# A squared-ReLU channel mixer with seven half-size products per block in place of eight

## The chip, the core and the metric

The kernel runs on one NeuronCore of a Trainium2 chip. Its engines work side by side, each through its own queue in order: TensorE (PE; its weight loads are shown as PEld), VectorE (DVE), ScalarE (ACT), GpSimd (POOL), and SyncE (SP), whose queue issues the transfers. The metric is device time in microseconds, the median of several runs.

## The reference

One step of a one-layer encoder over 576 tokens whose output is returned (512 of a prompt and 64 of a sample stream; 16 meta tokens more take part in attention). Two token mixers (differential attention, gated DeltaNet) are merged, projected and added to x. The part that the change touches is the last:

```python
h2 = _rmsnorm(x, p["norm2"])
x = x + jnp.square(jax.nn.relu(h2 @ p["w_up"])) @ p["w_down"]
```

with 1024 features, a hidden width of 4096, all in float32.

## The kernel before

All large products are one stream of tasks on PE. A task takes a block of 256 columns of a weight matrix over 1024 rows. The weights (`wr`, two transfers of 512 KB a task) are split into a high part `wh` (an ACT cast) and the remainder `wl` (a subtraction on DVE or POOL); activations likewise. A product of float32 quality is then three passes: high times high, high times low, low times high (`feat`).

In the channel mixer a task makes 256 features for 576 tokens: two halves of the features by two halves of the tokens, each 8 blocks of rows by 3 passes, that is 4 x 24 = 96 matmuls of a 128x128 weight tile against 288 tokens. There are 16 tasks of `w_up` (`up_task`, PSUM tiles `pg_u`) and 16 of `w_down` (`down_tasks`, `pg_dn`, four quarters of the hidden width by four blocks of features). They are ordered with the first `up` task of the next quarter ahead of a quarter's `down` tasks.

The eviction of an `up` piece is four instructions on 288 tokens: ReLU times the token's norm (DVE, from PSUM to `ur`), a square (ACT), a cast to `uh` (ACT), and the remainder `ul` (DVE). The hidden values have ten buffers of each kind, so a task has many matmuls to go before its predecessor's values are wanted. The eviction of a `down` piece is one DVE addition to the residual `x1`.

Which engine gets what, and when, is decided as the program is written, by `Pace`, an estimate of each engine's time. `stream` puts a step of the next task's weights (`split_hi`, `split_lo`, `load`) between every eight matmuls; `drive` lets the chains (norms, evictions, output) go on beside it; `VG` gives an elementwise operation to DVE or POOL, whichever the estimate has done sooner. The queues are then fixed: an instruction waits in its queue for everything ahead of it. The lines are

```python
QUANTUM = 8     # products between two turns of the chains
wp = Tags(pace, ctx.enter_context(pool("weights")), wh=2, wl=2, wr0=1, wr4=1)
```

`token_norm` finds 1/sqrt of each token's mean square (`n2` tiles, PSUM tiles `pss` and `prs`); `write_y` turns the result back to tokens on PE (`pyo`) and stores it.

## Time and profile before

| | |
|---|---|
| median of 3 runs | 1376.14 us (1373.91 to 1378.1) |
| profiled execution, first to last instruction | 1370.9 us, so 5.2 us less than that median |
| PE busy / PEld busy | 1315.5 us (96%) / 1273.0 us (93%) |
| DVE / ACT / POOL busy | 700.1 us (51%) / 565.8 us (41%) / 260.6 us (19%) |
| channel mixer, first `pg_u` to last `pg_dn` | 951.01 to 1364.89 us: 413.9 us |

Only the mixer's 413.9 us are changed in what they compute; busy shares over the whole span say little about them. The profiled execution has no time of its own beside its span, so sums are made against the span and carried over to the median by the 5.2 us.

### The profile page before, as it was taken

Reading aid. Unit: us, or ns where it says so; the run is one execution under the profiler, and the core shown is the slowest. Engines: PE = TensorE matmul, PEld = TensorE weight load, DVE = VectorE, ACT = ScalarE, POOL = GpSimd, SP = SyncE. Lnnn points to the kernel's source line nnn. Section 1 sums busy time; section 2 is a strip of 40 time slices with the busy share of each in tenths; the row PEclk is TensorE's granted clock in tenths of the full one; section 3 lists DMA queues with packets and bytes.
Section 4 is the critical chain, followed back from the end, with each engine's and each line's share of the span. In section 5 each row is a group of like instructions: output and inputs, shape, how many; then the busy total and the mean of one; then the engine's idle time right before and its main releaser. Section 6 shows DMA issues by size and latency. Waiting matters only on the chain.

```text
span 1370.9 us, 25684 instructions
## 1 busy us (share of the span) xinstructions
PE 1315.5 (96%) x10365; PEld 1273.0 (93%) x10365; DVE 700.1 (51%) x1556; ACT 565.8 (41%) x1368; POOL 260.6 (19%) x244
## 2 busy tenths in 40 slices
PE   3999999999999999998799899999999999999998
PEld 3999999999999999997688799999999999999998
DVE  5766999434377424278867743535332233233232
ACT  3556554433752333355566532323431331331321
POOL 5101422200230000243232101200220220320300
PEclk9999999999999999999999999999999999999999
DMA  6314243522644413774453157532222222222231
GB/s 171 93 47 133 88 126 122 154 91 73 210 120 132 138 59 93 236 225 149 122 172 101 67 171 257 191 98 78 77 87 70 91 93 72 83 93 78 78 110 52
DMA packets 163946, 161.06 MB, mean 117 GB/s; under 512 B 23546, under 2 KB 143628, under 8 KB 163828
## 3 DMA queue, kind: packets, MB, share of 16 engines
...
## 4 chain that ended last, share of the span: by engine, by line
PE 84%; DVE 8%; ACT 4%; DMA 3%; issue 1%; SPq 1%; ACTq 0%; DVEq 0%
PE pg_dn L164 15%; PE pg_u L164 15%; PE pg_a L164 10%; PE pg_d L164 9%; PE pg_g L164 6%; PE pg_z L164 4%; PE pg_o L164 4%; PE pg_ba L164 4%; PE pg_bb L164 3%; PE ppo L164 2%; DVE sc L164 2%; PE po L164 1%; ACT djk L164 1%; PE psc L164 1%; PE pwT L164 1%
## 5 line engine op out<-in xcount | busy, mean ns | idle before, releaser
L164 PE MATMUL pg_dn<-ul,wh_dn 128*128 128x288 f32 x512 | 151.6, 296 | 0.0
L164 PE MATMUL pg_dn<-uh,wh_dn 128*128 128x288 f32 x512 | 151.6, 296 | 0.0
L164 PE MATMUL pg_u<-h2h,wh_u 128*128 128x288 f32 x512 | 151.4, 296 | 0.0
L164 PE MATMUL pg_u<-h2h,wl_u 128*128 128x288 f32 x512 | 151.2, 295 | 0.0
L164 PE MATMUL pg_u<-h2l,wh_u 128*128 128x288 f32 x512 | 151.2, 295 | 0.0
L164 PE MATMUL pg_dn<-uh,wl_dn 128*128 128x288 f32 x512 | 151.1, 295 | 0.0
L164 PE MATMUL pg_a<-wh_a,hh 128*128 128x256 f32 (+1 forms) x480 | 136.3, 284 | 0.9 <-ACT sq L164 0.9
L164 PE MATMUL pg_a<-wh_a,hl 128*128 128x256 f32 (+1 forms) x480 | 136.2, 284 | 0.0
L164 PE MATMUL pg_a<-wl_a,hh 128*128 128x256 f32 (+1 forms) x480 | 135.6, 282 | 0.0
L164 PE MATMUL pg_d<-hl,wh_d 128*128 128x336 f32 (+1 forms) x384 | 116.5, 303 | 0.4 <-DVE hl L164 0.3
L164 PE MATMUL pg_d<-hh,wh_d 128*128 128x336 f32 (+1 forms) x384 | 116.2, 303 | 0.6 <-ACT hh L164 0.5
L164 PE MATMUL pg_d<-hh,wl_d 128*128 128x336 f32 (+1 forms) x384 | 115.9, 302 | 0.0
L164 POOL TENSOR_TENSOR wl_u<-wr_u,wh_u 128x1024 fp32r<-128x1024 f32 x22 | 52.8, 2401 | 260.5 <-ACT wh_u L164 260.5
L164 DVE TENSOR_TENSOR x<-x,pg_dn 128x288 f32<-128x288 f32 x64 | 29.1, 454 | 132.5 <-PE pg_dn L164 132.5
L164 PEld LDWEIGHTS pg_u<-h2h,wh_u 128*128 128x128 f32 x512 | 96.5, 189 | 0.1
L164 PEld LDWEIGHTS pg_u<-h2l,wh_u 128*128 128x128 f32 x512 | 96.5, 189 | 0.0
L164 PEld LDWEIGHTS pg_u<-h2h,wl_u 128*128 128x128 f32 x512 | 96.5, 188 | 0.0
L164 PEld LDWEIGHTS pg_dn<-uh,wl_dn 128*128 128x128 f32 x512 | 96.3, 188 | 0.0
L164 PEld LDWEIGHTS pg_dn<-uh,wh_dn 128*128 128x128 f32 x512 | 96.1, 188 | 0.0
L164 PEld LDWEIGHTS pg_dn<-ul,wh_dn 128*128 128x128 f32 x512 | 96.1, 188 | 0.0
L164 PEld LDWEIGHTS pg_a<-wh_a,hh 128*128 128x128 f32 (+1 forms) x480 | 86.6, 180 | 2.1 <-ACT sq L164 1.5
L164 PEld LDWEIGHTS pg_a<-wh_a,hl 128*128 128x128 f32 (+1 forms) x480 | 86.7, 181 | 0.7 <-issue 0.6
...
## 6 DMA issues: line engine op xcount, KB each, us to landing
wr_u<-in_w_up_dram SPq DMA_DIRECT2D x32, 512.0 KB, 3.7
wr_dn<-in_w_down_dram SPq DMA_DIRECT2D x32, 512.0 KB, 3.5
wr_d<-in_w_in_dram SPq DMA_DIRECT2D x24, 512.0 KB, 4.1
wr_a<-in_w_in_dram SPq DMA_DIRECT2D x24, 512.0 KB, 4.1
wr_g<-in_w_in_dram SPq DMA_DIRECT2D x16, 512.0 KB, 4.7
...
wr_z<-in_w_in_dram SPq DMA_DIRECT2D x8, 512.0 KB, 3.8
```

The costliest lines, as they stand in the source:

```text
L164: r = f(*a, **kw)
```

## The change

Each task is read as a product of 2x2 blocks: two halves of the block's columns by two interleaved halves of its rows (weights a11, a12, a21, a22), and two halves of the rows by two halves of the tokens. Seven products of sums of these (Strassen's algorithm in Winograd's form) take the place of eight. Each of the seven is 4 blocks of rows by 3 passes, 12 matmuls of 128x128 against 288 tokens: 84 a task.

- The seven products are called by number and run in the order 1, 6, 7, 5, 2, 4, 3. They use four PSUM tiles: `pa` (1, then 2 added to it), `pb` (6), `pc` (7, then 4), `pd` (5, then 3). A tile is evicted before its second product is added.
- Weights (`seven_steps`): four sums of 512 elements (`s1` to `s4`, into the tile `s` and in place in `wr`), then 3 1/2 casts and 3 1/2 subtractions of 1024 where there were 2 of each. They come as two blocks: the first (products 1, 6, 7, 5) is made during the task before, the second (2, 4, 3) during the task itself.
- Activations (`combine`): each pair of feature tiles is kept as seven pieces. Four results in `r` give three pieces at once (a cast and a subtraction of 864); four subtractions of 288 in place give the other four (a cast and a subtraction of 1152).
- An `up` task now evicts seven products into `uw` and `r`, one set of buffers for all tasks. When product 3 is out, the chain `squares` does ReLU and squares on 576 elements twice and then `combine`. Product 5 of the next task is evicted only after that chain has been written (`after`).
- The order is four `up` tasks, then four `down` tasks, four times. The first `up` task, and the first `down` task of each group, take the last of the four pairs late (`LATE`).
- Some constants and scratch tiles move to a pool that ends before the merge; there are no other changes of substance before the mixer.

```diff
+        def seven_steps(i):
...
+            def s1():
+                (_, a21), (_, a22) = quarters(0), quarters(1)
+                st["s"] = late["wx"].tile([P, 4, 256], F32, name=f"s_{tasks[i].nm}", tag="ws")
+                VG(2.1, 512).tensor_tensor(st["s"][:, :, 0:128], a21, a22, ALU.add)
+            def s2():
+                VG(2.1, 512).tensor_tensor(st["s"][:, :, 128:256], st["s"][:, :, 0:128], quarters(0)[0], ALU.subtract)
+            def s3():
+                a11, a21 = quarters(0)
+                VG(2.1, 512).tensor_tensor(a21, a11, a21, ALU.subtract)
+            def s4():
+                a12 = quarters(1)[0]
+                VG(2.1, 512).tensor_tensor(a12, a12, st["s"][:, :, 128:256], ALU.subtract)
+            def hi(b, a, x, n=256):
+                if a == 0:
+                    block(i)
+                S.copy(wts[i][b]["wh"][:, 4 * a:4 * a + 4, 0:n], x()[:, :, 0:n])
+            def lo(b, a, x, n=256, tag=None):
+                w = wts[i][b]
+                lower(w["wl"][:, 4 * a:4 * a + 4, 0:n], x()[:, :, 0:n], w["wh"][:, 4 * a:4 * a + 4, 0:n])
+                if tag:
+                    load(tag)
+            r0, r1, s = lambda: raw[i, 0], lambda: raw[i, 1], lambda: st["s"]
+            before = [(None, s1), (None, s2), (None, s3),
+                      (room, lambda: hi(0, 0, r0)), (None, lambda: lo(0, 0, r0, tag="wr0")),
+                      (None, lambda: hi(0, 1, s)), (None, lambda: lo(0, 1, s))]
+            own = [(room, lambda: hi(1, 0, r1)), (None, lambda: lo(1, 0, r1)), (None, s4),
+                   (None, lambda: hi(1, 1, r1, 128)), (None, lambda: lo(1, 1, r1, 128, tag=odd_tag[i]))]
+            return before, own
...
+    SEVEN = {1: (0, 0, 0, "a"), 6: (0, 3, 6, "b"), 7: (0, 1, 3, "c"), 5: (0, 2, 4, "d"),
+             2: (1, 0, 1, "a"), 4: (1, 1, 5, "c"), 3: (1, 2, 2, "d")}
+    EVEN = [(p, range(4)) for p in SEVEN]
+    LATE = [(p, range(3)) for p in (1, 6, 7, 5)] + [(p, range(3, 4)) for p in (1, 6, 7, 5)] + [(p, range(4)) for p in (2, 4, 3)]
+    def seven(xs, nm, evac, late_pair=None, after=None):
+        def body(w):
+            ps, n = {}, 0
+            for p, ks in LATE if late_pair else EVEN:
+                blk, m, x, bk = SEVEN[p]
+                if bk not in ps:
+                    pl, tag = (pg, "pg") if bk in "ac" else (pt, "pt")
+                    ps[bk] = pl.tile([P, 512], F32, name=f"p{bk}_{nm}", tag=tag)[:, :TH]
+                for k in ks:
+                    while late_pair and k == 3 and late_pair not in done:
+                        yield False
+                    wh, wl = (w[blk][y][:, 4 * (m // 2) + k, (m % 2) * P:(m % 2) * P + P] for y in ("wh", "wl"))
+                    xh, xl = (y[:, x] for y in xs[k])
+                    for i, (ww, xx) in enumerate(((wh, xh), (wh, xl), (wl, xh))):
+                        TE.matmul(ps[bk], ww, xx, start=p in (1, 6, 7, 5) and k == 0 and i == 0, stop=k == 3 and i == 2,
+                                  skip_group_check=True)
+                        n += 1
+                        if k == 3 and i == 2:
+                            w[0]["free"] = p in (5, 2, 4, 3)
+                            while p == 5 and after and after not in done:
+                                yield False
+                            evac(p, ps[bk])
+                        elif n < 6:
+                            continue
+                        n = 0
+                        yield
+        return body
+    def combine(hi, lo, r):
+        S.copy(hi[:, 0:3], r[:, 1:4])
+        V.tensor_tensor(lo[:, 0:3], r[:, 1:4], hi[:, 0:3].bitcast(F32), ALU.subtract)
+        yield
+        e = VG(2.1, 4 * TH)
+        e.tensor_tensor(r[:, 1], r[:, 0], r[:, 1], ALU.subtract)
+        e.tensor_tensor(r[:, 0], r[:, 3], r[:, 0], ALU.subtract)
+        e.tensor_tensor(r[:, 3], r[:, 3], r[:, 1], ALU.subtract)
+        e.tensor_tensor(r[:, 2], r[:, 2], r[:, 3], ALU.subtract)
+        yield
+        S.copy(hi[:, 3:7], r)
+        V.tensor_tensor(lo[:, 3:7], r, hi[:, 3:7].bitcast(F32), ALU.subtract)
...
     def up_task(i):
-        def evac(h, ps, a, b):
-            j = 2 * i + h
-            if a == 0:
-                uh[j] = ml.tile([P, TQ], F32R, name=f"uh{j}", tag="uh", bufs=10)
-                ul[j] = ml.tile([P, TQ], F32R, name=f"ul{j}", tag="ul", bufs=10)
-                gts["u"] = gp.tile([P, TQ], F32, name=f"ur{j}", tag="gth")
-            r = gts["u"]
-            V.scalar_tensor_tensor(r[:, a:b], ps, 0.0, late["rstd2"][:, a:b], ALU.max, ALU.mult)
-            S.activation(r[:, a:b], r[:, a:b], AF.Square)
-            split(uh[j][:, a:b], ul[j][:, a:b], r[:, a:b])
+        hl = []
+        def evac(p, ps):
+            r = late["r"]
+            if p == 1:
+                us[i % 4] = hl[:] = [ml.tile([P, 7, TH], F32R, name=f"u{x}{i}", tag=f"u{x}{i % 4}") for x in "hl"]
+                if i == 0:
+                    late["uw"], late["G"] = gp.tile([P, 2, TH], F32, name="uw", tag="gth"), {}
+                S.copy(late["uw"][:, 0], ps)
+            elif p == 6:
+                V.tensor_tensor(late["uw"][:, 1], late["uw"][:, 0], ps, ALU.add)
+            elif p == 7:
+                V.tensor_tensor(late["uw"][:, 0], late["uw"][:, 1], ps, ALU.add)
+            elif p == 5:
+                V.tensor_tensor(r[:, 3], late["uw"][:, 0], ps, ALU.add)
+            elif p == 2:
+                S.copy(r[:, 1], ps)
+            elif p == 4:
+                V.tensor_tensor(r[:, 2], late["uw"][:, 1], ps, ALU.add)
+            else:
+                V.tensor_tensor(r[:, 0], late["uw"][:, 1], ps, ALU.add)
+                chains.insert(0, Chain(squares(i, *hl)))
         def body(w):
-            yield from feat(late["h2h"], late["h2l"], f"u{i}", evac, after="mlp")(w)
-        return Task(f"u{i}", w_up[0], i * 256, body, has("h2") if i == 0 else None)
+            yield from seven(late["h2"], f"u{i}", evac, "h23" if i == 0 else None, f"u{i - 1}" if i else None)(w)
+            if i == 15:
+                done.add("up")
+        return Task(f"u{i}", w_up[0], i * 256, body, has("mlp", "h20", "h21", "h22") if i == 0 else None, seven=True)
+    def squares(i, hi, lo):
+        r = late["r"]
+        while "norm2" not in done:
+            yield
+        for h, x in ((0, r[:, 1:3]), (1, r[:, 0:4:3])):
+            R = late["rstd2"][:, None, h * TH:h * TH + TH].to_broadcast([P, 2, TH])
+            V.scalar_tensor_tensor(x, x, 0.0, R, ALU.max, ALU.mult)
+            S.activation(x, x, AF.Square)
+            yield
+        yield from combine(hi, lo, r)
+        done.add(f"u{i}")
     def down_tasks(qd):
         out = []
         for c in range(4):
-            def evac(h, ps, a, b, c=c):
-                j = 2 * c + h
+            def evac(p, ps, c=c):
                 x1 = late["x1"]
-                V.tensor_tensor(x1[:, j, a:b], x1[:, j, a:b], ps, ALU.add)
-                if qd == 3 and h == 1 and b == TQ:
+                if qd == 0 and p == 1 and c % 2 == 0:
+                    late["G"][c] = gp.tile([P, 2, TH], F32, name=f"G{c}", tag="gth")
+                g = late["G"][c - c % 2][:, c % 2]
+                if p == 1 and qd == 0:
+                    S.copy(g, ps)
+                    return
+                x11, x12, x21, x22 = (x1[:, 2 * c + h, t * TH:t * TH + TH] for h in range(2) for t in range(2))
+                x = {1: g, 6: g, 7: x22, 5: x22, 2: x11, 4: x21, 3: x12}[p]
+                V.tensor_tensor(x, x, ps, ALU.add)
+                if qd == 3 and p == 6:
+                    x2 = x1[:, 2 * c + 1].rearrange("p (a b) -> p a b", a=2)
+                    VG(2.1, TQ).tensor_tensor(x2, x2, g[:, None, :].to_broadcast([P, 2, TH]), ALU.add)
+                    VG(2.1, TH).tensor_tensor(x12, x12, g, ALU.add)
+                if qd == 3 and p == 3:
                     chains.append(Chain(write_y(c)))
             def body(w, c=c, evac=evac):
-                ks = range(8 * qd, 8 * qd + 8)
-                yield from feat([uh[k] for k in ks], [ul[k] for k in ks], f"dn{qd}{c}", evac)(w)
-            out.append(Task(f"dn{qd}{c}", w_down[0][qd * 1024:(qd + 1) * 1024], c * 256, body))
+                yield from seven([us[k] for k in range(4)], f"dn{qd}{c}", evac, f"u{4 * qd + 3}" if c == 0 else None)(w)
+            out.append(Task(f"dn{qd}{c}", w_down[0][qd * 1024:(qd + 1) * 1024], c * 256, body,
+                            has(*[f"u{4 * qd + k}" for k in range(3)]), seven=True))
         return out
...
-    for i in range(16):
-        tasks.append(up_task(i))
-        if i >= 4 and i % 4 == 0:
-            tasks += down_tasks(i // 4 - 1)
-    tasks += down_tasks(3)
+    for qd in range(4):
+        tasks += [up_task(i) for i in range(4 * qd, 4 * qd + 4)] + down_tasks(qd)```

The queues show what this does to the order. VectorE before, in the middle of the `up` tasks (`ur`, `uh`, `ul`: a hidden tile and its two parts):

```order
L164 SCALAR_TENSOR_TENSOR ur_11435<-pg_u_11395,rstd_10191 128x288
L164 TENSOR_TENSOR ul_11434<-ur_11435,uh_11433 128x288
L164 SCALAR_TENSOR_TENSOR ur_11435<-pg_u_11440,rstd_10191 128x288
L164 TENSOR_TENSOR ul_11434<-ur_11435,uh_11433 128x288
L164 SCALAR_TENSOR_TENSOR ur_11499<-pg_u_11469,rstd_10191 128x288
```

And now, during the last `up` task of the second group (`pb_u`, `pc_u`, `pd_u` are its products; `r`, `uh_12608`, `ul_12609` belong to the task before it; `wl` and `s` are weights):

```order
L165 SCALAR_TENSOR_TENSOR r<-r,rstd_10196 128x576
L165 TENSOR_TENSOR wl_u_12730<-wr_u_12533,wh_u_12729 128x1024
L165 TENSOR_TENSOR uw<-uw,pb_u_12742 128x288
L165 SCALAR_TENSOR_TENSOR r<-r,rstd_10196 128x2x288
L165 TENSOR_TENSOR wl_u_12730<-wr_u_12533,wh_u_12729 128x4x128
L165 TENSOR_TENSOR uw<-uw,pc_u_12760 128x288
L165 TENSOR_TENSOR s_dn_12775<-s_dn_12775,wr_dn_12718 128x4x128
L165 TENSOR_TENSOR ul_12609<-r,uh_12608 128x864
L165 TENSOR_TENSOR r<-r 128x288 x4
L165 TENSOR_TENSOR ul_12609<-r,uh_12608 128x1152
L165 TENSOR_TENSOR r<-uw,pd_u_12777 128x288
L165 TENSOR_TENSOR wl_dn_12810<-wr_dn_12718,wh_dn_12809 128x1024
```

The eviction of product 5 (`r<-uw,pd_u`) now stands behind the whole of the last task's chain; three more evictions and one more `wl` follow before the round starts again.

ScalarE before, at the same place (`wh`: weights):

```order
L164 ACTIVATE ur_11567<-ur_11567 128x288
L164 CAST uh_11565<-ur_11567 128x288
L164 CAST wh_u_11618<-wr_u_11523 128x1024
L164 ACTIVATE ur_11631<-ur_11631 128x288
L164 CAST uh_11629<-ur_11631 128x288
```

And now, in the round shown for VectorE:

```order
L165 ACTIVATE r<-r 128x576
L165 CAST wh_u_12729<-wr_u_12533 128x1024
L165 COPY uw<-pa_u_12722 128x288
L165 CAST wh_u_12729<-wr_u_12533 128x4x128
L165 ACTIVATE r<-r 128x2x288
L165 CAST uh_12608<-r 128x864
L165 CAST uh_12608<-r 128x1152
L165 CAST wh_dn_12809<-wr_dn_12718 128x1024
```

A square and its cast no longer follow each other: weight casts stand between the squares and the hidden casts, and VectorE's `wl` needs the `wh` behind a square. GpSimd's queue has three weight sums of 512 in such a round (`s4` of this task, `s1` and `s3` of the next), where it had subtractions of 1024 before.

## Rows read from the trace of the kernel before

**Rows 1.** The page's first part: busy time, share, instructions.

```profile
span 1370.9 us, 25684 instructions
...
PE 1315.5 (96%) x10365; PEld 1273.0 (93%) x10365; DVE 700.1 (51%) x1556; ACT 565.8 (41%) x1368; POOL 260.6 (19%) x244
```

**Rows 2.** Chain that ended last, 850 to 1371 us: start, length, what.

```profile
951.01 3.16 PE pg_u L164 x24
...
960.26 57.48 PE pg_u L164 x432
...
1068.71 50.92 PE pg_u L164 x384
...
1324.46 0.22 PE pyo L164 x2
...
1364.89 0.55 PE pyo L164 x5
```

**Rows 3.** Waits, 850 to 1371 us: total, times, longest.

```profile
DVE x L164 <- PE pg_dn L164: 132.5, 64, 2.8
...
DVE ur L164 <- PE pg_u L164: 80.3, 61, 2.7
```

**Rows 4.** DVE groups, 700 to 1371 us: busy, mean ns, idle before.

```profile
L164 DVE TENSOR_TENSOR wl_dn<-wr_dn,wh_dn 128x1024 fp32r<-128x1024 f32 x24 | 29.3, 1219 | 0.0
L164 DVE TENSOR_TENSOR x<-x,pg_dn 128x288 f32<-128x288 f32 x64 | 29.1, 454 | 132.5 <-PE pg_dn L164 132.5
...
L164 DVE SCALAR_TENSOR_TENSOR h2l<-x,vec,h2h 128x576 fp32r<-128x576 f32 x8 | 6.5, 815 | 3.4 <-ACT h2h L164 3.4
...
L164 DVE TENSOR_TENSOR sqa<-sqa,sq 128x576 f32<-128x576 f32 x4 | 3.0, 750 | 0.0
```

**Rows 5.** ACT groups, 700 to 1371 us.

```profile
L164 ACT CAST wh_dn<-wr_dn 128x1024 fp32r<-128x1024 f32 x32 | 32.5, 1046 | 75.5 <-PE pg_dn L164 75.5
...
L164 ACT ACTIVATE sq<-x 128x576 f32<-128x576 f32 x7 | 4.7, 671 | 0.0
```

**Rows 6.** POOL groups, whole span.

```profile
L164 POOL TENSOR_TENSOR wl_u<-wr_u,wh_u 128x1024 fp32r<-128x1024 f32 x22 | 52.8, 2401 | 260.5 <-ACT wh_u L164 260.5
...
L164 POOL TENSOR_TENSOR sqa<-sqa,sq 128x576 f32<-128x576 f32 x3 | 4.5, 1488 | 48.1 <-ACT sq L164 48.1
```

**Rows 7.** DVE in order of time, 1072 to 1096 us: start, length.

```profile
1075.11 0.46 DVE L164 SCALAR_TENSOR_TENSOR ur<-pg_u,rstd 128x288 f32<-128x288 f32 x1 [1.30 <-PE pg_u L164]
1076.54 0.52 DVE L164 TENSOR_TENSOR ul<-ur,uh 128x288 fp32r<-128x288 f32 x1 [0.98 <-ACT uh L164]
```

**Rows 8.** ACT in order of time, same stretch.

```profile
1075.60 0.45 ACT L164 ACTIVATE ur<-ur 128x288 f32<-128x288 f32 x1 [1.34 <-DVE ur L164]
1076.08 0.44 ACT L164 CAST uh<-ur 128x288 fp32r<-128x288 f32 x1
```

**Rows 9.** Stretches: engines' busy us (x instructions), PEclk, DMA share, GB/s.

```profile
896.00:897.50 1.50, 0.00 (x0) 0.00 (x0) 0.84 (x2) 0.00 (x0) 0.00 (x0) 1.00 0.03 11
...
899.00:900.00 1.00, 1.00 (x5) 1.00 (x5) 0.10 (x1) 1.00 (x3) 0.00 (x0) 0.50 0.00 0
```

**Rows 10.** PE in order of time, 892 to 903 us.

```profile
899.31 0.44 PE L164 MATMUL pg_o<-mxh,wl_o 128*128 128x288 f32 x1
899.55 0.44 PE L164 MATMUL pg_o<-mxh,wh_o 128*128 128x288 f32 x1
```

**Rows 11.** DVE in order of time, 770 to 786 us.

```profile
776.07 2.24 DVE L164 SCALAR_TENSOR_TENSOR mx<-mx,lam 128x1 f32<-128x1 f32 x1
...
780.87 0.22 DVE L164 SCALAR_TENSOR_TENSOR mx<-mx,lam 128x1 f32<-128x1 f32 x1
```

**Rows 12.** POOL in order of time, 765 to 790 us.

```profile
775.92 4.67 POOL L164 TENSOR_TENSOR wl_bb<-wr_bb,wh_bb 128x1024 fp32r<-128x1024 f32 x2 [24.45 <-ACT wh_bb L164]
```

**Rows 13.** POOL in order of time, 1072 to 1096 us.

```profile
1074.34 2.41 POOL L164 TENSOR_TENSOR wl_u<-wr_u,wh_u 128x1024 fp32r<-128x1024 f32 x1 [2.15 <-ACT wh_u L164]
```

**Rows 14.** The page's sixth part, a transfer: KB, us to landing.

```profile
wr_u<-in_w_up_dram SPq DMA_DIRECT2D x32, 512.0 KB, 3.7
```

More of the change, by code (lines that the diff above doesn't have):

```diff
@@ L318, in stream @@
-        for k in (0, 4):
-            load(0, k)
-        yield False
-        for k in (0, 4):
-            split_hi(0, k)
-            split_lo(0, k)
+        raw, wts, held = {}, {}, []
+        users = {"wr0": deque(), "wr4": deque(), "wrx": deque()}
+        for i, t in enumerate(tasks):
+            if t.src is not None:
+                odd = "wr4" if not t.seven or sum(x.seven for x in tasks[:i]) % 2 else "wrx"
+                users["wr0"].append((i, 0, "wr0"))
+                users[odd].append((i, 1, odd))
@@ new lines, in stream, with load, go @@
+        odd_tag = {i: tag for q in ("wr4", "wrx") for i, _, tag in users[q]}
+        def load(tag):
+            if not users[tag]:
+                return
+            i, k, _ = users[tag].popleft()
+            t = tasks[i]
+            pl = late["wx"] if tag == "wrx" else wp
+            def go():
+                raw[i, k] = pl.tile([P, 4, 256], F32, name=f"wr_{t.nm}{k}", tag=tag)
+                src = t.src[:, t.c0:t.c0 + 256]
+                if t.seven:
+                    src = src.rearrange("(k t p) n -> t p k n", t=2, p=P)[k]
+                else:
+                    src = src[4 * k * P:(4 * k + 4) * P].rearrange("(k p) n -> p k n", p=P)
+                Q.dma_start(raw[i, k], src)
+            pace.stores.append((pl.when(tag, 1), ((i, k),), go))
+            if "start" not in done:
+                pace.flush(key=(i, k))
+            if k == 0 and odd_tag[i] == "wrx" and "wx1" not in done:
+                done.add("wx1")
+                load("wrx")
@@ L324, in stream, with before @@
+        for tag in ("wr0", "wr4"):
+            load(tag)
+        yield False
+        own = {}
+        def before(i):
+            if i >= len(tasks) or tasks[i].src is None:
+                return []
+            if not tasks[i].seven:
+                return plain_steps(i)
+            b, own[i] = seven_steps(i)
+            return b
+        first = before(0)
+        for k in (0, 1, 2, 4):
+            first[k][1]()
         yield False
-        for k in (0, 4):
-            load(1, k)
+        for k in (3, 5):
+            first[k][1]()
@@ L1444, in write_y @@
         yield
+        while "y" not in late:
+            yield
         for t, (c0, n) in enumerate(QTILES):
@@ L1471, in stream_step_kernel @@
     tasks += br_b_tasks() + br_a_tasks() + out_tasks()
-    for i in range(16):
-        tasks.append(up_task(i))
-        if i >= 4 and i % 4 == 0:
-            tasks += down_tasks(i // 4 - 1)
-    tasks += down_tasks(3)
+    for qd in range(4):
+        tasks += [up_task(i) for i in range(4 * qd, 4 * qd + 4)] + down_tasks(qd)
     main = stream(tasks)
@@ L1506, in stream_step_kernel @@
             xp = ctx.enter_context(pool("x1"))
+            late["wx"] = Tags(pace, xp)
             late["x1"] = xp.tile([P, KC, TQ], F32, name="x1")
             late["rstd2"] = xp.tile([P, TQ], F32, name="rstd2")
-            late["h2h"] = [xp.tile([P, TQ], F32R, name=f"h2h{j}") for j in range(KC)]
-            late["h2l"] = [xp.tile([P, TQ], F32R, name=f"h2l{j}") for j in range(KC)]
+            late["r"] = xp.tile([P, 4, TH], F32, name="r")
+            rp = Tags(pace, xp)
             chains.append(Chain(residual()))
             drive(has("br_a", "resid"))
-        with pool("resid", side="right") as rp_:
-            done.add("tail")
-            rp = Tags(pace, rp_, sq2=2, dg=5)
-            drive(lambda: "norm2" in done and not chains)
+        h2_cm = pool("h2")
+        h2 = h2_cm.__enter__()
+        late["h2"] = [[h2.tile([P, 7, TH], F32R, name=f"h2{x}{j}", tag=f"h2{x}{j}") for x in "hl"] for j in range(4)]
+        done.add("tail")
+        drive(has("out"))
     with pool("mlp", side="right") as ml:
         done.add("mlp")
+        drive(has("up", "u15"))
+        h2_cm.__exit__(None, None, None)
+        late["y"] = ctx.enter_context(pool("y"))
         drive(has(*[f"y{c}" for c in range(4)]))
```

166 lines of the change are left out of this document (92 added, 74 removed).

## The prediction

> **What bounds the kernel now.** I read the shares of busy time first, then the chain that ended last, the waits, and the durations by form. TensorE is busy 96% of the span and its weight loads 93%, VectorE 51% [rows 1]. In the mixer the chain runs through matmuls almost alone: 384 of them take 50.92 us, 0.1326 us each [rows 2], so a task of 96 takes 12.73 us. VectorE's longest waits are for those products [rows 3], each shorter than a group of 24 matmuls (3.2 us): it has time over. The mixer lasts from 951.01 to 1364.89 us, 413.9 us [rows 2].
>
> So if nothing else came in the way, 32 tasks of 84 in place of 96 matmuls would save 384 x 0.1326 = 50.9 us. What decides is whether the elementwise work of an `up` task, in the order in which it is now queued, fits into 84 x 0.1326 = 11.1 us.
>
> **Durations.** VectorE: 288 elements 0.454 us, 576 0.750 (0.815 with three operands), 1024 1.219 [rows 4]. From the first and the last, 1.04 ns an element: 864 takes 1.05 us, 1152 1.35, 512 0.69. ScalarE: 576 0.671, 1024 1.046 [rows 5], so 864 0.91, 1152 1.15, 512 0.62. GpSimd: 576 1.488, 1024 2.40 [rows 6], so 512 about 1.36. From one engine to the next it takes 0.03 to 0.05 us: the ReLU ends at 1075.57, the square starts at 1075.60; the cast at 1076.08 ends at 1076.52, `ul` starts at 1076.54 [rows 7, 8].
>
> **VectorE's sum for one `up` task.** Two ReLUs 1.6, three `wl` of 1024 3.66, one of 512 0.69, one weight sum 0.69, five evictions 2.27, the pieces 1.05 + 1.35, four subtractions in place that each wait for the last, some 0.475 each: 1.9. That is 13.2 us against TensorE's 11.1: even without a wait VectorE would be the bound there. In a `down` task it is six or seven evictions and some 5 us of weights, 8 to 9 us, which fits.
>
> **The waits in a round.** I walk the queue of the round shown in the change, time 0 where the first ReLU starts, right behind the eviction of product 3.
> - ReLU to 0.8. ScalarE squares to 1.5, and only behind it casts `wh` to 2.5; VectorE's `wl` needs that: 2.5 to 3.7. Idle 1.7.
> - GpSimd may now make `s4`, 3.8 to 5.15. VectorE evicts product 6 to 4.1 and asks for its second ReLU, which I let GpSimd hold until 5.15 (below): done 5.8. ScalarE casts the half `wh` to 5.8, squares to 6.5, casts 864 to 7.4.
> - GpSimd's `s1` runs 5.8 to 7.15 and holds `wl` of 512: done 7.7. Eviction of product 7 to 8.1. `s3` runs 7.7 to 9.0 and holds `s2`: done 9.6.
> - `ul` 864 to 10.5, the four subtractions to 12.4, ScalarE's cast of 1152 to 13.6 with VectorE idle, `ul` 1152 to 15.0.
> - Product 5 is evicted at 15.45. Only now may TensorE start product 3; products 2 and 4 have been done since 9.7. It has stood for 5.8 us, so its 12 matmuls come at the low clock: after a stretch without a matmul the granted clock read 0.50, the 1.2 GHz level [rows 9], and matmuls started 0.24 us apart [rows 10]. 12 x 0.24 = 2.9, to 18.4. Meanwhile `wl`, an eviction, `wl` end at 18.1.
> - Product 3's eviction follows. The round is 18.4 to 18.9 us; I take 18.5, against 12.73 before and 11.1 hoped for.
>
> **Whether GpSimd holds VectorE.** A VectorE operation on one element a partition lasts 2.24 us beside a GpSimd operation, 0.22 without [rows 11]; it began 0.15 us after GpSimd's first of two and ended at 778.31, that one at about 775.92 + 4.67/2 = 778.26 [rows 11, 12]. An operation with an operand in PSUM was not stretched: 0.46 us inside a GpSimd subtraction of 2.41 [rows 7, 13]. So I hold the operations with both operands in SBUF, in the order in which they asked. The bounds: no hold at all, as at the PSUM operand, makes the round 16.6 us; GpSimd's queue running through before VectorE's turn, 19.4. One such meeting in the trace is not a law for a round with three of them. The Trainium skill (SBUF — State Buffer, Who interferes with whom) states one: a VectorE instruction with two SBUF inputs and a GpSimd instruction that reads SBUF exclude each other for the whole instruction, and the one that was issued first goes first. By it the round is 18.5; by the PSUM row taken for all, 16.6.
>
> **A group of four `up` and four `down` tasks.**
> - The first `up` task has no chain before it: 11.1 + 0.5 (eviction) + 1.3 (its ReLU waits for a GpSimd `wl` of 2.4 us) = 12.95.
> - Three rounds: 55.5.
> - The chain of the fourth has no product to hide behind. TensorE runs 36 matmuls on the other three pairs (4.8 us), then waits for `ul` 1152: 14.5 from the ReLU. Then the 9 matmuls of the last pair at the low clock, 2.2, and products 2, 4, 3 partly so, 5.4.
> - Three more `down` tasks at 11.1: 33.4. Their weights are just in time: after product 5 (6.4) and `s3` the first cast is ready at 9.1, `wl` at 10.4, and GpSimd's other `wl` at 12.8, wanted at 13.0. A slip costs tenths.
> - Sum 124.0, four times 496. The first group adds some 8 us: TensorE waits about 4.5 us for the last pair of `h2`, goes on at the low clock (1.0), and the mean squares' products and VectorE's small operations on them delay the first chain by 2.5. The old kernel pays 6.1 us at that place within its 413.9 (24 matmuls from 951.01, the next at 960.26 [rows 2]). The turning of the output, 20 x 0.22 us [rows 2], stays: 4.3.
>
> After: 496 + 8 + 4.3 = 508, 94 us more than 413.9. Transfers carry the same bytes and land in 3.7 us [rows 14]; the first half of a task's weights is asked for behind the `wl` that ends at 10.4, and its first sum stands 6 us later, so they cost nothing. The moved constants, and the few instructions that change place before the mixer, I cost at nothing, because matmuls cover them there; uncovered, at one wait like the longest of [rows 3], 2.8 us, either way. The span becomes 1370.9 + 94 = 1465, and with the 5.2 us to the median 1470 us.
>
> **Rivals.**
> - A, no hold by GpSimd. 4 x (11.6 + 49.8 + 12.85 + 2.2 + 5.4 + 33.4) = 461, and 12.3: 473, 60 more, 1436 us. For it the PSUM row; against it [rows 11, 12].
> - B, waits between engines hidden, so that only VectorE's sum counts: 4 x (11.6 + 39.6 + 9 + 2.2 + 5.4 + 33.4) + 12.3 = 417, 3 more, 1379 us. Against it, the in-order queues: `wh` stands behind the square on ScalarE.
> - C, the other side: TensorE stays the bound, because the order lets the chain of one task run beside all seven products of the next. It is the change's saving, 51 us, and gives 1325 us. It decides once a round fits in 11.1 us. For it the 96% of [rows 1]; against it the 13.2 us of VectorE. The Trainium skill (Perfetto Trace Analysis, Identifying the Most-Contended Engine) judges TensorE's headroom by the share of its weight loads and would have the fullest engine relieved first; by that rule this is the result, and the 93% agrees with the rule for the kernel before.
> - D, worse: GpSimd's queue goes first (19.4) and the `down` tasks' weights come a microsecond late each: 4 x (12.95 + 58.2 + 15.5 + 2.2 + 5.4 + 37) + 12.3 = 537, 123 more, 1500 us.
>
> **How the numbers follow.** The forecast's own mechanism (hold, 18.5 a round give or take 1, so 1458 to 1485) gets 0.72, A 0.12, B 0.05, C 0.04, D 0.07. The range goes from just under A to D: 1425 to 1500; it leaves out B and C. A measurement here can tell 0.3%, 4 us. Faster: C and a little of B, 0.05; the same: the middle of B, 0.02; slower: the rest, 0.93.
>
> **What would show it.** Right: in the second to fourth `up` task of each group, TensorE's wait before product 3 (`pd_u`) for VectorE near 6 us and a round near 18.5; VectorE's waits for `wh` and for `uh` near 1.7 and 1.2; two-operand VectorE instructions stretched beside GpSimd; `down` tasks after a group's first at 11.1; about 10 us of waiting inside each group's first `down`; granted clock below 1 in the mixer. Wrong: a chain that is still almost all matmuls (C); rounds of 16.6 with nothing stretched (A) or of 13 (B); `down` tasks that wait for `wl` (D). If the loss lies before 951 us, the reading is wrong altogether.

## The result, and the profile after

The kernel after the change takes 1475.26 us (median of 4 runs, 1472.58 to 1478.55), the kernel before 1375.12 in the same session: ratio 1.0734, 95% interval 1.0708 to 1.0760. Slower by 100 us, with 384 matmuls fewer. Times here are medians of runs at like granted clocks; one run of e9 at a clock of 0.82 took 1505.87 us and is left out of its median.

The first part of the page after (answers to [rows 1]):

```profile
span 1475.4 us, 25481 instructions
...
PE 1313.0 (89%) x9981; PEld 1261.1 (85%) x9981; DVE 948.4 (64%) x1830; ACT 638.3 (43%) x1417; POOL 339.5 (23%) x304
```

TensorE is as long busy as before although it does less: part of it runs at the low clock (the mean granted clock of the profiled execution is 0.944, 0.988 before). The whole loss is in the mixer: its first product starts at 953.8 us (951.0 before) and its last ends at 1469.2, 515.4 us in place of 413.9. The waits after, from 940 us on (total, times, longest):

```profile
PE pd_u L165 <- DVE r L165: 67.5, 12, 7.4
...
DVE wl_u L165 <- ACT wh_u L165: 34.1, 24, 1.9
...
DVE ul L165 <- ACT uh L165: 22.4, 21, 1.7
```

In [rows 3] VectorE waited for products; now TensorE waits for VectorE, twelve times (the second to fourth `up` task of four groups), 5.6 us each, ahead of `pd_u`. One such round, VectorE in order of time (start, length):

```profile
1122.15 0.75 DVE L165 SCALAR_TENSOR_TENSOR r<-r,rstd 128x576 f32<-128x576 f32 x1
...
1124.65 1.22 DVE L165 TENSOR_TENSOR wl_u<-wr_u,wh_u 128x1024 fp32r<-128x1024 f32 x1 [1.75 <-ACT wh_u L165]
...
1126.15 1.70 DVE L165 SCALAR_TENSOR_TENSOR r<-r,rstd 128x576 f32<-128x576 f32 x1
1127.93 1.64 DVE L165 TENSOR_TENSOR wl_u<-wr_u,wh_u 128x512 fp32r<-128x512 f32 x1
...
1129.85 1.40 DVE L165 TENSOR_TENSOR s_u<-s_u,wr_u 128x512 f32<-128x512 f32 x1
1131.18 1.05 DVE L165 TENSOR_TENSOR ul<-r,uh 128x864 fp32r<-128x864 f32 x1
1132.26 1.94 DVE L165 TENSOR_TENSOR r<-r 128x288 f32<-128x288 f32 x4
1135.41 1.36 DVE L165 TENSOR_TENSOR ul<-r,uh 128x1152 fp32r<-128x1152 f32 x1 [1.22 <-ACT uh L165]
1136.87 0.45 DVE L165 TENSOR_TENSOR r<-uw,pd_u 128x288 f32<-128x288 f32 x1
...
1140.73 0.45 DVE L165 TENSOR_TENSOR r<-uw,pd_u 128x288 f32<-128x288 f32 x1 [0.77 <-PE pd_u L165]
1141.10 0.75 DVE L165 SCALAR_TENSOR_TENSOR r<-r,rstd 128x576 f32<-128x576 f32 x1
```

From ReLU to ReLU it is 18.95 us, as in the other rounds behind a group's first. A group's first round takes 19.87 (21.6 in the first group): its first ReLU is held by a low part that GpSimd is making.

```profile
1102.28 1.69 DVE L165 SCALAR_TENSOR_TENSOR r<-r,rstd 128x576 f32<-128x576 f32 x1
```

In the round shown, the second ReLU, the low part of 512 and the sum `s` are twice as long as without GpSimd (0.75, 0.69 and 0.69 us, see e1). GpSimd in the same stretch:

```profile
1125.95 1.29 POOL L165 TENSOR_TENSOR wr_u<-wr_u,s_u 128x512 f32<-128x512 f32 x1 [14.20 <-DVE wl_u L165]
1127.32 1.70 POOL L165 TENSOR_TENSOR s_u<-wr_u,wr_u 128x512 f32<-128x512 f32 x1
1129.09 1.61 POOL L165 TENSOR_TENSOR wr_u<-wr_u 128x512 f32<-128x512 f32 x1
```

Each long VectorE instruction ends 0.55 to 0.61 us after the GpSimd one that it met (1127.85 after 1127.24, 1129.57 after 1129.02, 1131.25 after 1130.70). TensorE behind the eviction of product 5:

```profile
1137.47 0.58 PE L165 MATMUL pd_u<-h2h,wh_u 128*128 128x288 f32 x1 [5.62 <-DVE r L165]
1137.85 0.45 PE L165 MATMUL pd_u<-h2l,wh_u 128*128 128x288 f32 x1
1138.09 0.45 PE L165 MATMUL pd_u<-h2h,wl_u 128*128 128x288 f32 x1
```

0.24 us apart, as in [rows 10], at the level that the granted clock shows from 1137.47 us on, 0.50 (1.2 GHz):

```profile
1137.47:1140.49 3.02, 3.02 (x13) 3.02 (x13) 2.49 (x3) 0.73 (x1) 0.00 (x0) 0.50 0.25 82
```

Last the chain through a group's first `down` task (start, length, what; compare the unbroken matmuls of [rows 2]):

```profile
1167.69 1.73 DVE ul L165
...
1171.42 1.16 ACT uh L165
...
1172.60 1.37 DVE ul L165
...
1174.02 0.85 PE pb_dn L165 x2
...
1176.31 2.88 PE pa_dn L165 x12
...
1182.69 1.60 PE pa_dn L165 x12
```

The fourth `up` task's chain stands bare there; the task takes from 1159.4 to 1182.7 us, the next one 11.1.

### The profile page after: what moved, and what is told of

It is laid out like the page before. It is cut to its first block, busy times and chain, and to the rows that moved or that the text cites. A ratio compares the mean times of both kernels' runs of the same rounds, so it can differ in the third digit from the quotient of the medians.

```text
span 1475.4 us, 25481 instructions
## 1 busy us (share of the span) xinstructions
PE 1313.0 (89%) x9981; PEld 1261.1 (85%) x9981; DVE 948.4 (64%) x1830; ACT 638.3 (43%) x1417; POOL 339.5 (23%) x304
## 3 DMA queue, kind: packets, MB, share of 16 engines
q8 instruction: 78, 1.28, 0.4%
## 4 chain that ended last, share of the span: by engine, by line
PE 63%; issue 14%; DVE 9%; POOL 5%; ACT 5%; DMA 4%; SPq 1%; POOLq 0%; DVEq 0%; ACTq 0%
PE pg_a L165 10%; PE pg_d L165 8%; PE pg_g L165 6%; PE pg_z L165 4%; PE pg_ba L165 4%; PE pg_o L165 3%; PE pa_dn L165 3%; PE pd_dn L165 3%; PE pc_dn L165 3%; PE pg_bb L165 3%; POOL wr_u L165 2%; PE ppo L165 2%; DVE sc L165 2%; PE pb_dn L165 2%; DMA bias_d<-bv_d 1%
## 5 line engine op out<-in xcount | busy, mean ns | idle before, releaser
L165 PE MATMUL pg_a<-wh_a,hh 128*128 128x256 f32 (+1 forms) x480 | 136.4, 284 | 2.3 <-ACT sq L165 2.3
L165 PE MATMUL pg_a<-wh_a,hl 128*128 128x256 f32 (+1 forms) x480 | 136.3, 284 | 0.0
L165 PE MATMUL pg_a<-wl_a,hh 128*128 128x256 f32 (+1 forms) x480 | 135.5, 282 | 0.0
L165 PE MATMUL pg_d<-hh,wh_d 128*128 128x336 f32 (+1 forms) x384 | 116.4, 303 | 0.6 <-ACT hh L165 0.5
L165 PE MATMUL pg_d<-hl,wh_d 128*128 128x336 f32 (+1 forms) x384 | 116.5, 303 | 0.4 <-DVE hl L165 0.3
L165 PE MATMUL pg_d<-hh,wl_d 128*128 128x336 f32 (+1 forms) x384 | 116.2, 303 | 0.0
L165 PE MATMUL pd_u<-h2h,wh_u 128*128 128x288 f32 x128 | 46.8, 365 | 67.5 <-DVE r L165 67.5
L165 PEld LDWEIGHTS pd_u<-h2h,wh_u 128*128 128x128 f32 x128 | 30.6, 239 | 70.0 <-ACT r L165 70.0
L165 PEld LDWEIGHTS pg_a<-wh_a,hh 128*128 128x128 f32 (+1 forms) x480 | 86.5, 180 | 3.4 <-ACT sq L165 2.8
L165 ACT CAST wh_dn<-wr_dn 128x1024 fp32r<-128x1024 f32 (+1 forms) x48 | 43.5, 906 | 104.8 <-POOL wr_dn L165 52.7
L165 PEld LDWEIGHTS pg_a<-wh_a,hl 128*128 128x128 f32 (+1 forms) x480 | 86.6, 180 | 0.7 <-issue 0.6
L165 PEld LDWEIGHTS pg_a<-wl_a,hh 128*128 128x128 f32 (+1 forms) x480 | 86.5, 180 | 0.5 <-issue 0.2
L165 DVE TENSOR_TENSOR wl_u<-wr_u,wh_u 128x1024 fp32r<-128x1024 f32 (+1 forms) x48 | 59.9, 1247 | 33.7 <-ACT wh_u L165 33.1
L165 PE MATMUL pg_g<-hh,wh_g 128*128 128x288 f32 x256 | 79.1, 309 | 0.0
L165 PE MATMUL pg_g<-hh,wl_g 128*128 128x288 f32 x256 | 78.6, 307 | 0.0
L165 PE MATMUL pg_g<-hl,wh_g 128*128 128x288 f32 x256 | 78.3, 306 | 0.0
L165 PEld LDWEIGHTS pg_d<-hl,wh_d 128*128 128x128 f32 x384 | 73.2, 191 | 1.7 <-DVE hl L165 1.0
L165 PEld LDWEIGHTS pg_d<-hh,wh_d 128*128 128x128 f32 x384 | 73.3, 191 | 1.3 <-ACT hh L165 1.1
L165 PEld LDWEIGHTS pg_d<-hh,wl_d 128*128 128x128 f32 x384 | 73.5, 191 | 0.7 <-issue 0.6
L165 DVE SCALAR_TENSOR_TENSOR cv_d<-pre_d,vec,cv_d 128x595 f32<-128x595 f32 x72 | 61.6, 861 | 15.9 <-ACT cv_d L165 9.1
L165 ACT CAST wh_u<-wr_u 128x1024 fp32r<-128x1024 f32 (+1 forms) x48 | 43.3, 902 | 65.3 <-POOL wr_u L165 44.4
L165 DVE TENSOR_TENSOR wl_dn<-wr_dn,wh_dn 128x1024 fp32r<-128x1024 f32 (+1 forms) x47 | 53.2, 1132 | 27.3 <-ACT wh_dn L165 27.3
## 6 DMA issues: line engine op xcount, KB each, us to landing
wr_u<-in_w_up_dram SPq DMA_DIRECT2D x32, 512.0 KB, 4.0
wr_dn<-in_w_down_dram SPq DMA_DIRECT2D x32, 512.0 KB, 3.4
wr_d<-in_w_in_dram SPq DMA_DIRECT2D x24, 512.0 KB, 5.1
wr_a<-in_w_in_dram SPq DMA_DIRECT2D x24, 512.0 KB, 4.2
wr_g<-in_w_in_dram SPq DMA_DIRECT2D x16, 512.0 KB, 5.4
wr_z<-in_w_in_dram SPq DMA_DIRECT2D x8, 512.0 KB, 4.0
```

Source lines behind the costliest of these rows:

```text
L165: r = f(*a, **kw)
```

## Experiments

Theory: VectorE's queue, in its fixed order, sets the `up` tasks' pace, by its work, by what GpSimd holds and by its waits for ScalarE's casts. Rivals: GpSimd is harmless; the one buffer `r` alone is to blame; TensorE's low clock is; the seven products are bad everywhere. All times are medians, to be held against 1475 us (after) and 1373 to 1375 (before, beside them).

**e1.** GpSimd's share of the weights to VectorE (all four sums, and the low parts):

```diff
-                VG(2.1, 512).tensor_tensor(st["s"][:, :, 0:128], a21, a22, ALU.add)
+                V.tensor_tensor(st["s"][:, :, 0:128], a21, a22, ALU.add)
```

> All sums and low parts of the weights of the seven-product tasks are made on VectorE; GpSimd makes none of them in the mixer. Theory of the forecast: GpSimd's three sums are no gift, because each holds back a VectorE operation with two operands in SBUF (beside them the 576-wide ReLU took 1.70 us where it takes 0.75 alone, the 512-wide low part 1.64, the sum of 512 1.40 against some 0.69). Put on VectorE they cost 3 x 0.69 = 2.1 us and give back 0.95 + 0.95 + 0.71 = 2.6, so the round stays at 18.4 to 19.0 us, no two-operand instruction is stretched, and the time is 1475 us, give or take 6. Rival: the long instructions are long for another reason and GpSimd's work is free; then the round grows by the 1.4 to 2.1 us that are added on the chain, 17 to 25 us in twelve rounds, and some more at the groups' ends: 1495 to 1505 us.

1482.28 us, ratio 1.0793 (1.0762 to 1.0825), a little over the range. VectorE in the second round of a group:

```profile
1122.54 0.75 DVE L165 SCALAR_TENSOR_TENSOR r<-r,rstd 128x576 f32<-128x576 f32 x1
...
1127.69 0.69 DVE L165 TENSOR_TENSOR wl_u<-wr_u,wh_u 128x512 fp32r<-128x512 f32 x1 [0.32 <-ACT wh_u L165]
...
1129.26 0.75 DVE L165 SCALAR_TENSOR_TENSOR r<-r,rstd 128x576 f32<-128x576 f32 x1
1129.93 0.69 DVE L165 TENSOR_TENSOR s_u<-s_u,wr_u 128x512 f32<-128x512 f32 x1
1131.71 1.06 DVE L165 TENSOR_TENSOR ul<-r,uh 128x864 fp32r<-128x864 f32 x1 [1.10 <-ACT uh L165]
...
1137.79 0.68 DVE L165 TENSOR_TENSOR wr_u<-wr_u 128x512 f32<-128x512 f32 x1
1139.63 1.23 DVE L165 TENSOR_TENSOR wl_u<-wr_u,wh_u 128x1024 fp32r<-128x1024 f32 x1 [1.16 <-ACT wh_u L165]
...
1142.63 0.75 DVE L165 SCALAR_TENSOR_TENSOR r<-r,rstd 128x576 f32<-128x576 f32 x1
```

With GpSimd's sums gone nothing is stretched, so it was GpSimd that made the three instructions long. But the round is not unchanged: the second and third of a group take 20.09 us (18.95 after the change), only the first is shorter (18.6 to 19.1 in the second to fourth group, 19.87 after). The twelve rounds are 5.8 us longer together (238.5 us in place of 232.7), and so is the profiled span (1481.1 in place of 1475.4): the loss lies in the rounds. The theory counted 2.6 us given back against 2.1 of work. What is new are waits for ScalarE's casts, 1.10 us for `uh`, as the second ReLU now stands behind two more sums, and 1.16 for `wh`, whose sum VectorE makes only behind the chain. So what GpSimd holds is not what is won when it goes; in this order its sums are worth some 0.5 us a round (5.8 over twelve), between the theory's nothing and the rival's 1.4 to 2.1. The hold's worth by itself is not shown.

**e2.** Two buffers `r`, no wait for the last chain:

```diff
-            r = late["r"]
+            r = late["rr"][i % 2]
...
-            yield from seven(late["h2"], f"u{i}", evac, "h23" if i == 0 else None, f"u{i - 1}" if i else None)(w)
+            yield from seven(late["h2"], f"u{i}", evac, "h23" if i == 0 else None, f"u{i - 2}" if i > 1 else None)(w)
```

> The buffer r is doubled, so that the eviction of product 5 is queued where the product ends and not behind the chain of the task before; to make room the low parts of the third and fourth pair of the up projection's input share one tile, so those values are wrong. Theory of the forecast: the order of the queue, not VectorE's sum alone, sets the 18.95 us round; without it the round falls to what VectorE has to do, 13.2 us and the 2.6 us that GpSimd holds it, 15.8 us. Three rounds in four groups then save 12 x 3.1 = 37 us, the wait in each group's first down task stays: 1438 us, 1425 to 1450. Rival, the wait for the buffer is the whole loss: TensorE becomes the bound again with 11.1 us a round, 12 x 7.8 = 94 us less, 1381 us. Second rival, VectorE is so full that order does not matter: 1475 us.

1473.94 us: my theory's 1438 missed; the time is the second rival's. In the second group the four `up` tasks take 63.0 us (68.8 after), but the first `down` task waits as much longer: what is done earlier on TensorE is not done earlier on VectorE. The planner also gave GpSimd low parts of 1024, which met the subtractions and a low part:

```profile
1108.56 3.75 DVE L165 TENSOR_TENSOR r<-r 128x288 f32<-128x288 f32 x4
...
1116.38 2.47 DVE L165 TENSOR_TENSOR ul<-r,uh 128x1152 fp32r<-128x1152 f32 x1
...
1133.93 4.80 DVE L165 TENSOR_TENSOR r<-r 128x288 f32<-128x288 f32 x4
```

**e5.** Both edits:

> The two edits of e1 and e2 together: r is doubled (with the low parts of the third and fourth pair in one tile, so those values are wrong) and VectorE makes all sums and low parts of the seven-product tasks. Alone, e1 gave 1482 and e2 1474 us. In e2 the rounds came sooner, but GpSimd's low parts and sums stood beside VectorE's four subtractions (3.75 and 4.80 us in place of 1.94) and the first down task waited for what had been put off: 16.7 us up to its last pair became 23 to 25. Theory: VectorE's queue is the bound of the whole group, in work and in what GpSimd holds; with neither the wait for the buffer nor GpSimd, an up task costs VectorE 13.2 + 3 x 0.69 = 15.3 us. From a group's start to the end of its last low part four such tasks and some 7 us of waits take 68 us, 82 in the kernel after the change and in e2: 4 x 14 = 56 us less, 1420 us, 1405 to 1440. Rival, the waits between ScalarE and VectorE in the chain set the pace and not VectorE's work: 1460 to 1480 us again.

1452.54 us, ratio to before 1.0565 (1.0515 to 1.0615): both together give 23 us where neither gave any, but not the 56 expected. In the second to fourth group the planner now put the four subtractions on GpSimd in nine chains, 3.86 to 4.70 us each where VectorE takes 1.94, so GpSimd was not out, and VectorE still waits 72.5 us for ScalarE's casts of `wh` and `uh`. How much each is of the missing 33 us stays open.

**e3 and e6.** 36 matmuls that nobody reads, ahead of product 3; e6 leaves them out in a group's first `up` task:

```diff
+                if p == 3 and after and int(nm[1:]) % 4:
+                    fill = pt.tile([P, 512], F32, name=f"fill_{nm}", tag="pt")[:, :TH]
+                    for f in range(36):
+                        TE.matmul(fill, w[1]["wh"][:, f % 4, 0:P], xs[f % 4][0][:, 0], start=True, stop=True)
```

> In each round 36 matmuls that nobody reads stand in TensorE's queue between product 4 and product 3, where it waits 5.6 us for VectorE. At 0.133 us each they take 4.8 us of that wait. Theory: product 3 is on the cycle that sets the round (eviction of 5, product 3, eviction of 3, ReLU), and its 12 matmuls came 0.24 us apart because TensorE had stood; without the stop they come 0.133 apart, 1.3 us less a round, in twelve rounds 16 us: 1459 us, with a wait of some 0.8 us left before product 3. Rival: the low clock there is hidden behind VectorE's own queue, which does two low parts and an eviction in the same 4 us: no change, 1475 us. Second rival, the fillers run late and delay product 3: above 1480 us.

1478.39 us; the edit was at fault, as it also delayed tasks that wait for nothing.

> As e3, but with fillers in the second to fourth up task of a group alone. In e3 they also stood in the first, where nothing is waited for, and cost 4.75 us there in three groups, while the round, from ReLU to ReLU, fell from 18.97 to 18.03 us. Theory: the low clock is on the cycle with 0.9 us a round; twelve rounds save 11 us: 1464 us, 1458 to 1470. Rival, what the rounds give is taken back by the wait in the first down task: 1475 us, as in e3.

1467.86 us, ratio 1.0674 (1.0643 to 1.0704), as expected. TensorE in e6:

```profile
1109.62 4.96 PE L165 MATMUL fill_u<-h2h,wh_u 128*128 128x288 f32 x36
1115.42 0.37 PE L165 MATMUL pd_u<-h2h,wh_u 128*128 128x288 f32 x1 [0.83 <-DVE r L165]
1115.62 0.30 PE L165 MATMUL pd_u<-h2l,wh_u 128*128 128x288 f32 x1
1115.76 0.29 PE L165 MATMUL pd_u<-h2h,wl_u 128*128 128x288 f32 x1
```

Behind its first matmul product 3 comes 0.13 us apart now. The second and third rounds of a group fell from 18.95 to 18.1 us, so the low clock was some 0.85 us of a round: a consequence of the wait that adds to it, not the cause.

**e9.** The first squaring behind the weight cast on ScalarE, by one turn's delay of the chain:

```diff
         while "norm2" not in done:
             yield
+        yield
```

> The kernel after the change with one thing moved: the first squaring of an up task's chain is queued behind the cast of the next weights on ScalarE, not ahead of it, so that VectorE finds the cast ready when its ReLU ends. In the kernel after the change VectorE waits there 1.7 us in every round (34.1 us in 24 waits for that cast), and the round is 18.95 us. Theory: VectorE's queue sets the round, its waits for ScalarE as much as its work, and the chain stands in it one behind the other; each round gives back 1.7 us, twelve of them 20 us: 1455 us, 1448 to 1462. Rival, another wait takes its place (the second ReLU waits for GpSimd, the next cast for the squaring): at most 5 us, 1470 us or more.

1447.1 us, ratio 1.0545 (1.0517 to 1.0573), just under the range: by the ratios 26 us from one line. VectorE:

```profile
1125.33 0.75 DVE L165 SCALAR_TENSOR_TENSOR r<-r,rstd 128x576 f32<-128x576 f32 x1
1126.00 1.22 DVE L165 TENSOR_TENSOR wl_u<-wr_u,wh_u 128x1024 fp32r<-128x1024 f32 x1
```

The 1.75 us between the two are gone; VectorE's total wait for `wh_u` fell from 34.1 to 12.5 us. The twelve rounds, 232.7 us after the change, take 213.8: 18.9 us less, where the theory had 20. Not all are shorter by the same (16.5 to 18.3 us, the first 21.6), as the planner also placed a sum or two otherwise. The other 8 us in the mixer lie outside the rounds and are not taken apart. The rival, by which another wait takes the place, had at most 5 us.

**e4.** Seven products in `down` alone; `up` in eight, its four quarters then combined:

```diff
+            r, q = late["rr"][i % 2], {(0, 0): 1, (0, TH): 0, (1, 0): 2, (1, TH): 3}[h, a]
...
+            V.scalar_tensor_tensor(r[:, q], ps, 0.0, late["rstd2"][:, a:b], ALU.max, ALU.mult)
+            S.activation(r[:, q], r[:, q], AF.Square)
+            if h == 1 and b == TQ:
+                chains.insert(0, Chain(pieces(i, *hl)))
```

> Seven products in the down projection alone. The up projection is done as in the kernel before, in eight; its four quarters are squared and then combined into the seven pieces that the down tasks need, with two buffers r and five of the pieces, and the first up task of the next group runs before the four down tasks, as in the kernel before. Theory: the seven products lose where a task's elementwise work is longer than its products. An up task of eight has 2.0 + 4.35 + 2.44 = 8.8 us of VectorE work in 12.73 us of products, a down task of seven 8 to 10 us in 11.1, so TensorE stays the bound in both: 16 x 12.73 + 16 x 11.1 = 381, some 6 us at the start as before, some 5 us for the last group's chain, 4.3 us for turning the output: 397 us in place of 413.9, about 1358 us. Rival: the combination costs as much as the products save, whatever the task (waits for its chain or a slower start): 1375 us or more.

1378.66 us, ratio 1.0027 (1.0005 to 1.0050): the rival's number. The `up` and the second to fourth `down` tasks are bound by matmuls, as the theory has it; the loss is in the first `down` tasks (4.5 us besides, since the mixer began later, see below). VectorE and GpSimd there:

```profile
1028.56 4.92 DVE L165 TENSOR_TENSOR r<-r 128x288 f32<-128x288 f32 x4
1033.41 0.44 DVE L165 TENSOR_TENSOR x<-x,pc_dn 128x288 f32<-128x288 f32 x1
...
1036.62 3.16 DVE L165 TENSOR_TENSOR ul<-r,uh 128x1152 fp32r<-128x1152 f32 x1 [0.30 <-ACT uh L165]
```

```profile
1029.02 1.28 POOL L165 TENSOR_TENSOR wl_dn<-wr_dn,wh_dn 128x512 fp32r<-128x512 f32 x1 [1.46 <-ACT wh_dn L165]
1030.25 1.49 POOL L165 TENSOR_TENSOR s_dn<-wr_dn,wr_dn 128x512 f32<-128x512 f32 x1
1031.81 1.36 POOL L165 TENSOR_TENSOR wr_dn<-wr_dn 128x512 f32<-128x512 f32 x1
```

The pieces of the next group's first `up` task, which nobody needs for four tasks, stand ahead of the eviction of product 7, and GpSimd holds them. TensorE waits for that eviction:

```profile
1033.91 0.61 PE L165 MATMUL pc_dn<-uh,wh_dn 128*128 128x288 f32 x1 [3.76 <-DVE x L165]
```

**e8 and e12.** e4 with the weights' sums and low parts on VectorE (e8), and `e = V` in `combine` too (e12):

> As e4 with the first of e7's two edits alone: no sum and no low part of the weights on GpSimd, the chain left where it was. Theory: of the 7 us that e4 loses at each first down task, GpSimd's hold is 3.0 us in the subtractions and 1.8 us in the low part; without it product 4 waits at most 1 us and the clock stays: 3 x 5 = 15 us less than e4, 1364 us. Rival: the chain itself, 4.35 us of VectorE in a task that has only some 1 us to spare, is the cause: 1375 to 1380 us as e4.

1377.01 us. This settles nothing: the planner moved the four subtractions to GpSimd, and VectorE's sums beside them took 0.93 to 1.28 us in place of 0.69:

```profile
1024.45 5.53 POOL L165 TENSOR_TENSOR r<-r 128x288 f32<-128x288 f32 x4 [79.07 <-DVE ul L165]
```

> As e8, and the four subtractions on the pieces are on VectorE too. In e8 they had moved to GpSimd, where they took 5.53 us beside VectorE's sums and low parts and the last low part of the pieces came late; so e8 did not take GpSimd out of the first down task. Here it is out, and the chain stays where it was. Theory: the chain alone is dear: in that task VectorE now has weights 4.35 + sums 2.76 + evictions 2.6 + chain 4.34 = 14.0 us against 11.1 of products, so some 3 us too many, with a piece at the low clock, in each of three groups: 9 to 12 us more than e7's 1362, that is 1371 to 1374; the remainder of e4's 1379 is what GpSimd's hold cost. Rival, the chain costs nothing if VectorE does it without GpSimd beside it: 1362 to 1365 us. Second rival, GpSimd made no difference at all: 1377 us or more.

1371.92 us, ratio 0.9982 (0.9964 to 1.0001), as expected. With GpSimd out of those stretches 7 us of e4 are gone.

**e7.** e8, and the late-needed pieces spread over the second and fourth `down` task:

```diff
+        steps = combine(hi, lo, late["rr"][i % 2])
+        for c in (1, 3, 3):
+            while late_ and f"go{i // 4 - 1}{c}" not in done:
+                yield
+            next(steps, None)
+            yield
```

> As e4 (seven products in the down projection alone), with two edits: VectorE makes all sums and low parts of the down tasks' weights, and the pieces of the first up task of the next group, which stands between two groups and is needed four tasks later, are made in three steps within the second and the fourth down task instead of all at once in the first. In e4 that chain and GpSimd met in each group's first down task: the four subtractions took 4.92 us there (1.93 elsewhere) and a low part 3.16 (1.36), product 4 waited 3.8 us for an eviction queued behind them and two products came at the low clock, some 7 us in each of three groups. Theory: without that, 21 us less than e4's 1379: 1358 us, 1350 to 1366, faster than the kernel before. Rival: with its sums VectorE has 9.6 to 10.2 us of work in a down task of 11.1 and ScalarE's casts in between, so the down tasks now wait in every task: 1370 us or more.

1361.78 us, ratio 0.9908 (0.9879 to 0.9938): 0.9% faster than the kernel before, a small gain but clear of its interval. GpSimd is not out here: it makes the four subtractions of three chains (5.14 to 5.50 us), so the place of the chain counts more than the engine. The stretch from 1250 to 1300 us, mostly `up` tasks, and the same of the kernel after (busy us of PE, PEld, DVE, ACT, POOL, then granted clock, DMA share, GB/s):

```profile
1250.00:1300.00 50.00, 50.00 (x378) 50.00 (x377) 31.11 (x47) 19.83 (x27) 0.00 (x0) 1.00 0.28 85
```

```profile
1250.00:1300.00 50.00, 32.02 (x192) 30.35 (x192) 37.91 (x46) 18.44 (x25) 13.80 (x9) 0.79 0.17 53
```

The kernel of e7 saves 192 matmuls, 25.5 us at 0.1326, and keeps 11. Of the rest some 8 us go in the last group, whose first `down` task has a bare chain ahead of it, and 2 in each of the two middle groups (97.5 us where four tasks of 12.73 and four of 11.1 make 95.3).

**e10.** e7, the last `up` task's pieces made one by one as the quarters come:

> As e7, and for the last up task alone the seven pieces are made one by one as their quarters come (two pieces and their low parts ahead of the last quarter, the piece that product 6 needs next), in place of three large steps behind the last quarter. In e7 the last group's first down task waits 5.2 us for the first pieces between its third and fourth pair and then has the low clock for a product and a half. Theory: from the last quarter's ReLU to the piece for product 6 it is now 0.45 + 0.45 + 0.4 + 0.45 + 0.47 + 0.4 + 0.45 = 3.1 us, less than the 4.8 us of the other pairs: the wait and the low clock go, 6 us less than e7's 1362: 1356 us. Rival: the small pieces cost VectorE more in sum and the first down task's weights come late, no gain: 1360 to 1364 us.

1362.20 us: no gain. The wait has only changed its name. TensorE's longest wait in e7 and in e10:

```profile
PE pb_dn L165 <- ACT uh L165: 4.6, 1, 4.6
```

```profile
PE pa_dn L165 <- DVE G L165: 5.2, 1, 5.2
```

The small pieces delay the second weight block and the eviction behind it: the rival.

**e11.** Seven products in `up` alone; the chain ends in two splits:

```diff
-        yield from combine(hi, lo, r)
+            split(hi[:, :, h * TH:h * TH + TH], lo[:, :, h * TH:h * TH + TH], x)
```

> Seven products in the up projection alone: the chain of an up task is two ReLUs, two squarings and two splits, with no pieces to combine; the down projection has eight products and its order is that of the kernel before (the next group's first up task ahead of the four down tasks). Here 16 x 1.6 = 25 us of matmuls are saved too. Theory: it is the up tasks that lose. VectorE has two ReLUs 1.6, weights 4.35, sums about 0.7 with two to three on GpSimd, five evictions 1.9 to 2.3, two low parts of 576 1.5, so 10 us, with 2.6 us that GpSimd holds it and 2 to 3 us of waits for ScalarE's casts: 14.5 to 15.5 us a round where eight products took 12.73, so about 16 x 2.3 = 37 us slower: 1410 us, 1395 to 1425. Rival: without the pieces the chain fits beside the products, TensorE stays the bound, 1350 to 1365 us as for the down projection.

1405.48 us, ratio 1.0236 (1.0211 to 1.0261), in the range. The four `up` tasks of the second group take 11.1, 15.8, 13.9 and 13.5 us, where eight products took 12.73: the first has no chain before it, and the others lose 1.7 us on average, less than the 2.3 expected. Of the 29 us that the mixer is longer, some 13 lie in the first five `up` tasks. Even without pieces to combine, the `up` projection loses by seven products in this order of the queues (e9's edit was not tried on it); the `down` projection wins once its neighbours' chains are out of its way.

## Why the prediction was right

It said 1470 us (1425 to 1500), slower; 1475 was measured, and the mechanism is the one forecast. That the two lie 5 us apart is in part luck: in profiled spans it is 1465 against 1475.4, 7.4 us of it in the mixer and 2.8 before. The 5.2 us from the span to the median came from a fast profiled execution of the kernel before; after the change span and median are the same within 0.2 us.

- **The round.** 18.5 us taken, 18.95 measured in the second and third of a group. The first takes 19.87; what makes it longer, a ReLU of 1.69 us beside GpSimd's low part, the forecast had as 1.3 us in the task before. From the ReLU's start the trace has the first `wl` ending at 3.7 us (3.7 in the walk), the second ReLU at 5.7 (5.8), `wl` of 512 at 7.4 (7.7), `s2` at 9.1 (9.6), `ul` at 10.1 and 14.6 (10.5, 15.0), product 5's eviction at 15.2 (15.45). The end was put too short: the eviction of product 3 behind its 3.0 us of matmuls stood in the walk's text but not in the 18.5.
- **TensorE's wait** 5.6 us (5.8); VectorE's for `wh` 1.75 (1.7), for `uh` 1.22 (1.2).
- **GpSimd's hold.** Right in size, 0.95 + 0.95 + 0.71 us a round, and e1 shows that the stretching goes with GpSimd's sums (though no time is won by it). The rule of the Trainium skill (SBUF — State Buffer, Who interferes with whom) gave 18.5; the traces agree with it and rule out the 16.6 of rival A.
- **Groups.** The second and third 125.4 and 124.4 us (124.0), the first 136.8 (132), the last 128.8 with the output (128.3). The first is the largest miss: its first wait for VectorE was 7.4 us. From the fourth chain's ReLU to the end of the first `down` task it is 22.6 us (22.1).
- **Before the mixer** the edits were costed at nothing, 2.8 us either way; the mixer began 2.8 us later than before. In the other kernels here with nearly the same program up to there it began at 948.3 to 956.0, so this cannot be put down to the change.
- **What the prediction did not see:** which single cause to lift. By the walk, freeing `r` should have brought a round to VectorE's 15.8 us; e2 shows that it does not, since the queue's waits and GpSimd's hold fill what is freed; e1 shows the same of GpSimd's 2.6 us. The prediction's terms were right as a sum along one fixed order, not as savings one by one. Of the 5.7 us that separate VectorE's sum (13.2) from the round, the wait for `wh` is the one that a single edit lifted (e9).
- Rival C's rule (Trainium skill, Perfetto Trace Analysis, Identifying the Most-Contended Engine) would have had the fullest engine relieved. The weight loads' share fell from 93 to 85% and the time rose: here the work added on the second-fullest engine decided.
